# A bidirectional GLA and pooling block on one core: small vectors through ScalarE's queue, the first weights split before the features, output stores put off

## The chip, the core and the metric

The kernel runs on one core of a Trainium2 chip. Five engines work side by side, each through its own list of instructions in order: TensorE (PE; its weight loads are shown as PEld), VectorE (DVE), ScalarE (ACT), GpSimd (POOL) and SyncE (SP), which here only issues DMAs. An engine that meets an instruction whose semaphore has not been reached stands there, and everything behind it in its list stands too. The metric is the device time of one execution in microseconds (us). Lower is better.

## The reference

One layer on a sequence of 1024 tokens of 1024 features, in float32:

```python
h = rmsnorm(x, norm_mix[l])
proj = h @ w_in[l]
q, k, v, r, lr_f, lr_b, u, g_a, g_b = jnp.split(proj, split_points, axis=-1)
...
o = o_fwd + o_bwd                       # gated linear attention, 4 heads, both directions
o = o * lax.rsqrt(jnp.mean(o * o, axis=-1, keepdims=True) + EPS)
...
y_a = o @ w_branch_gla[l]
...
merged = jax.nn.sigmoid(g_a) * y_a + jax.nn.sigmoid(g_b) * y_b
x = x + merged @ w_out[l]
h2 = rmsnorm(x, norm_ffn[l])
gate, up = jnp.split(h2 @ w_ffn_in[l], 2, axis=-1)
x = x + (jax.nn.silu(gate) * up) @ w_ffn_out[l]
return rmsnorm(x, norm_final)
```

## The kernel before

All large products are made from a high and a low part of each operand: `split_to` casts a tile on ACT (line 196, outputs `wh`, `hh`, `oh`: high) and subtracts the cast from the source on DVE or POOL (line 197, outputs `wl`, `hl`, `ol`: low). Three matmuls (`products`, line 270) then stand for one. TensorE is busy nearly all the time, and the rest of the program is arranged beside it.

**Order of the work.** The program is written out by hand: each engine does its instructions in the order in which the Python code emits them. Work beside the products is emitted by `pump`, which is called after each group of three matmuls and counts their cost. `soon(delay, step)` puts a step into the list `put_off`; `pump` lowers all the delays, and emits steps from the front of the list only, so that a step whose delay has passed still waits for the one ahead of it. `Weights` puts the splits of a loaded weight block into the list `pending`.

**The start.** The sequence is normed tile by tile: `norm_x(t)` makes the mean square of 128 tokens on ACT (`norm_scale`, line 310), adds EPS on DVE (line 301), raises to the power -0.5 on POOL (line 302), scales on DVE (line 306, output `xn`), and loads tile t + 4 into the place of tile t. TensorE transposes `xn` (line 317, output `tr`), and `gain_and_split` makes the features of two tiles from it, four times, each on a pair of feature blocks: ACT writes the high part with the norm's gain (line 324, `hh`), DVE the low part (line 327, `hl`). The gains come from six small vectors that are loaded into the 40 rows of one tile `rows`, transposed at line 410 and copied to `cols`. The first product, `values(w, v, 0)`, needs the four parts of its weights (`raw`, loaded as four DMAs of 256 KB) split, and the features of tiles 0 and 1; the second, `values(w, v, 1)`, has the transposes of tiles 2 and 3 after its first three matmuls.

**DMA completion semaphores.** The framework has eight semaphores for the ends of DMAs, `DMAHW0` to `DMAHW7`. It hands them out in turn to the DMAs of the whole program, whichever queue issues them. A DMA that gets a semaphore for the second time first waits, in the queue that issues it, until the DMA that had it before has landed. The tables of order below show these waits in brackets.

**The end.** The last product, of the FFN's output, is made in seven steps p (`OUT_ORDER`), each over six pieces; a piece is loaded as `wor` and `gor` by SP (lines 1641, 1643 and 1644) and split as above. `collect` adds a finished sum to the residual (line 1753). After step p = 3 the tiles 0 to 3 are whole: `whole(m)` squares them, and `soon` emits the scale (2 units later), the final norm (`finish`, line 1724, 1.5 units later) and, within `finish`, the store of the tile (line 1727). Steps 7 and 4 follow and finish tiles 4 to 7 (lines 1742 to 1747).

Of the kernel before, what the change touches and what calls it, by code (L numbers as in the profile page):

```python
# [15 lines left out]
ALU = mybir.AluOpType  # L16

P = 128
# [16 lines left out]
EPS = 1e-6  # L35
# [16 lines left out]
def kernel(  # L52
# [20 lines left out]
    nc = tc.nc  # L73
    x, out = x[0], out[0]
# [16 lines left out]
    def name(s):  # L91
        count[0] += 1
        return f"{s}_{count[0]}"

    def slot(dtype=F32, shape=(2, HALF), s="slot"):
        return slots.tile([P, *shape], dtype, tag="slot", name=name(s))
# [7 lines left out]
    def vec(width, s="v"):  # L104
        return small.tile([P, width], F32, tag="vec", name=name(s), bufs=12)
# [4 lines left out]
    def as_f32(ap):  # L110
        return ap.bitcast(F32)
# [8 lines left out]
        out=keepf[:, :P], in_=keepf[:, :P], compare_op=ALU.is_ge, fill=0.0,  # L120
# [25 lines left out]
    pending, credit = [], [0.0]  # L146
# [4 lines left out]
    def soon(delay, *steps):  # L151
        put_off.extend([delay, step] for step in steps)
# [42 lines left out]
    def split_to(hi, lo, src, eng=nc.vector):  # L195
        nc.scalar.copy(hi, src)  # L196
        eng.tensor_tensor(lo, src, as_f32(hi), op=ALU.subtract)  # L197
# [13 lines left out]
    class Weights:  # L211
# [8 lines left out]
        def split(self, raw):  # L220
            hi = wts.tile(list(raw.shape), F32R, tag="wh", name=name("wh"))[:, :, :]
            lo = wts.tile(list(raw.shape), F32R, tag="wl", name=name("wl"))[:, :, :]
            split_to(hi, lo, raw[:, :, :], nc.gpsimd if hT.tiles else nc.vector)
            self.parts.append((hi, lo))

        def finish(self):
# [15 lines left out]
    def fetch():  # L242
        src = next(order, None)
        if src is not None:
            loaded.append(load(*src))

    def prepare():
        if not loaded:
            fetch()
        if loaded:  # L250
            ready.append(Weights(loaded.pop(0)))

            credit[0] = -2.0
# [44 lines left out]

    def rms_scale(ms, width, s):
        rs = vec(width, s)  # L300
        nc.vector.tensor_scalar(rs[:, :], ms, EPS, None, op0=ALU.add)
        nc.gpsimd.tensor_tensor(rs[:, :], rs[:, :], half_neg[:, :width], op=ALU.pow)
        return rs

# [3 lines left out]
    def norm_scale(xt, sq, s):  # L308
        ms = vec(1, s + "ms")
        nc.scalar.activation(sq[:, :], xt, AF.Square, scale=1.0 / 32.0, accum_out=ms[:, :])  # L310
        return rms_scale(ms[:, :], 1, s + "rs")

    def transpose_tile(ps, xt, i, kp):
        for kk in range(2):
            c = slice((2 * kk + i) * P, (2 * kk + i + 1) * P)
            k = 2 * kp + kk
            nc.tensor.transpose(ps[:, c], xt[:, k * P : (k + 1) * P], ident[:, :])  # L317

    def gain_and_split(ps, kp, t0, act, gain):
        c = slice((t0 % 4) * P, (t0 % 4 + 2) * P)  # L320
        both = range(2 * kp, 2 * kp + 2)
        srcs = [(ps[:, i * 2 * P : (i + 1) * 2 * P], gain[:, k : k + 1]) for i, k in enumerate(both)]
        for k, (src, g) in zip(both, srcs):
            nc.scalar.activation(act(k, t0 // 4)[0][:, c], src, AF.Copy, scale=g)
        for k, (src, g) in zip(both, srcs):
            hi, lo = act(k, t0 // 4)
            nc.vector.scalar_tensor_tensor(
                lo[:, c], src, g, as_f32(hi[:, c]), op0=ALU.mult, op1=ALU.subtract
            )
# [11 lines left out]
    xt = [slot(shape=(D,), s="x") for _ in range(4)]  # L341
    xn = [slot(shape=(D,), s="xn") for _ in range(4)]
    vec_rows = [(norm_mix, 8), (norm_ffn, 8), (gla_norm, 8), (pool_scale, 8), (b_decay_fwd, 4), (b_decay_bwd, 4)]
    n_rows = sum(n for _, n in vec_rows)
    rows = tmp.tile([n_rows, P], F32, tag="t2", name="rows")
    uraw = slot(F32, (HEADS, 2, DK), "uraw")
    lraw = slot(F32, (KT, 2 * RANK), "lraw")

    def load_x(t):
        nc.sync.dma_start(xt[t % 4][:, :], x[t * P : (t + 1) * P, :])  # L350

    def load_rows(at, v, n):
        nc.sync.dma_start(rows[at : at + n, :], v[0].rearrange("(j p) -> j p", p=P))

    def load_up(i, d, w):
        r = 2 * RANK * i + RANK * d
        nc.sync.dma_start(uraw[r : r + RANK, :, d, :], w[0].rearrange("r (h c) -> r h c", h=HEADS))

    load_x(0)
    load_rows(0, *vec_rows[0])  # L360
    load_x(1)
    for i in range(1, len(vec_rows)):
        load_rows(sum(n for _, n in vec_rows[:i]), *vec_rows[i])
    fetch()
    for t in (2, 3):
        load_x(t)
# [3 lines left out]
    hT = Activations("h")  # L370
# [32 lines left out]
    def value_slots():  # L403
        return [(slot(F32R, (4, DV), "vh"), slot(F32R, (4, DV), "vl")) for _ in range(2)]

    v = value_slots()
# [10 lines left out]
    for t in range(2):  # L417
        for kp, ps in enumerate(trs):
            transpose_tile(ps, xn[t], t, kp)
    prepare()  # L420
    for kp, ps in enumerate(trs):
        pending.pop(0)()
        gain_and_split(ps, kp, 0, hT, g_mix)
    w = take(ahead=False)
    norm_x(2)
# [203 lines left out]
    def attention(h, q, k):  # L629
# [153 lines left out]
        for n in range(NT):  # L783
# [24 lines left out]
            if n == 3:  # L808
                p = q_next
            yield 1.02  # L810
        rs = rms_scale(ms[:, :], NT, "ors")
        if h == HEADS - 1:
            o_heads[h] = o
# [20 lines left out]
    for h in range(HEADS):  # L834
# [4 lines left out]
        if h > 0:  # L839
            v = value_slots()  # L840
# [641 lines left out]
    def squares(t, ms, res, j):  # L1482
        nc.scalar.activation(
            res[:, COLS[j]], x2[t][:, COLS[j]], AF.Square, scale=1.0 / 32.0, accum_out=ms[:, j : j + 1]
        )

    def two_scale(ms):
        rs = vec(1, "n3rs")
        nc.vector.tensor_scalar(rs[:, :], ms[:, 0:1], ms[:, 1:2], EPS, op0=ALU.add, op1=ALU.add)
        nc.gpsimd.tensor_tensor(rs[:, :], rs[:, :], half_neg[:, :1], op=ALU.pow)  # L1490
        return rs
# [220 lines left out]
    def whole(t):  # L1712

        ms, res = vec(4, "n3ms"), slot(shape=(D,), s="res")
        for j in range(2):
            squares(t, ms, res, j)

        def scale():
            rs = two_scale(ms)
            soon(1.5, partial(finish, rs))  # L1720

        def finish(rs):
            for j in range(2):
                nc.vector.scalar_tensor_tensor(
                    res[:, COLS[j]], x2[t][:, COLS[j]], rs[:, :], gain_final[:, COLS[j]], op0=ALU.mult, op1=ALU.mult
                )
            nc.sync.dma_start(out[t * P : (t + 1) * P, :], res[:, :])

        soon(2, scale)

# [43 lines left out]
    for at, p in enumerate(OUT_ORDER):  # L1774
# [4 lines left out]
        for i in range(CLOSE if closing else n_of):  # L1779
            n = at * n_of + i  # L1780
# [50 lines left out]
```

## Time and profile before

| | |
|---|---|
| median of 3 runs | 1402.03 us (1400.65 to 1402.65) |
| the profiled execution | 1400.65 us, its span 1398.9 us |
| TensorE busy | 1368.4 us, 98% of the span |
| VectorE, ScalarE, GpSimd busy | 849.5, 625.6, 748.3 us |
| TensorE clock granted | 0.999 |
| DMA | 243.62 MB, mean 174 GB/s |

Times in the rows are us from the start of the span, durations of single instructions ns where it says so. A row of the timeline gives start, duration, engine, line, operation, output and inputs, and in brackets how long the engine had stood idle before it and what ended that. Rows of merged instructions carry their number as xN. Matmuls overlap each other, so that a merged row is shorter than their sum.

### The profile page before, as it was taken

Reading aid. Unit: us, or ns where it says so; the run is one execution under the profiler, and the core shown is the slowest. Engines: PE = TensorE matmul, PEld = TensorE weight load, DVE = VectorE, ACT = ScalarE, POOL = GpSimd, SP = SyncE. Lnnn points to the kernel's source line nnn. Section 1 sums busy time; section 2 is a strip of 40 time slices with the busy share of each in tenths; the row PEclk is TensorE's granted clock in tenths of the full one; section 3 lists DMA queues with packets and bytes.
Section 4 is the critical chain, followed back from the end, with each engine's and each line's share of the span. In section 5 each row is a group of like instructions: output and inputs, shape, how many; then the busy total and the mean of one; then the engine's idle time right before and its main releaser. Section 6 shows DMA issues by size and latency. Waiting matters only on the chain.

```text
span 1398.9 us, 18565 instructions
## 1 busy us (share of the span) xinstructions
PE 1368.4 (98%) x6677; PEld 1152.5 (82%) x6677; DVE 849.5 (61%) x1073; ACT 625.6 (45%) x1117; POOL 748.3 (53%) x558
## 2 busy tenths in 40 slices
PE   7999999999999999999999999999999999999997
PEld 6889898978888878788887788888888888888876
DVE  6256757567745975687875865556565556343363
ACT  6364655564233444455346633333333334453253
POOL 3242626031378456568665176666666667454354
PEclk9999999999999999999999999999999999999999
DMA  6212404341268667996515455554444447975461
GB/s 193 76 45 61 136 37 137 102 125 53 76 199 281 213 209 232 354 404 244 200 71 180 166 181 174 173 173 159 145 141 149 140 154 254 388 255 218 165 234 67
DMA packets 167612, 243.62 MB, mean 174 GB/s; under 512 B 10936, under 2 KB 98016, under 8 KB 167520
## 3 DMA queue, kind: packets, MB, share of 16 engines
q1 hardware_dynamic: 167520, 242.45, 51.3%
q8 instruction: 52, 0.85, 0.2%
q14 instruction: 40, 0.33, 0.1%
HBM read 164.55 MB, written 77.86 MB: 173 GB/s over the span
## 4 chain that ended last, share of the span: by engine, by line
PE 81%; DVE 7%; ACT 3%; issue 3%; POOL 3%; DMA 2%; SPq 0%; POOLq 0%; DVEq 0%; ACTq 0%
PE ps L270 74%; PE op L797 2%; POOL wl L197 1%; PE kv L270 1%; PE sc L733 1%; PE op L270 1%; PE tr L317 1%; DMA u_out<-uph 1%; DVE z L666 1%; PE ps L448 1%; DVE fs L866 0%; DMA gor<-g_out 0%; DMA wor<-t_out 0%; DVE so L725 0%; ACT wh L196 0%
## 5 line engine op out<-in xcount | busy, mean ns | idle before, releaser
L197 POOL TENSOR_TENSOR wl<-fs,wh 128x512 fp32r<-128x512 f32 x120 | 166.1, 1388 | 164.8 <-ACT wh L196 139.5
L270 PE MATMUL ps<-gl,wh 128*128 128x512 f32 x616 | 239.8, 389 | 0.9 <-DVE gl L1423 0.9
L270 PE MATMUL ps<-gh,wh 128*128 128x512 f32 x616 | 240.4, 390 | 0.0
L270 PE MATMUL ps<-gh,wl 128*128 128x512 f32 x616 | 239.7, 389 | 0.0
L197 POOL TENSOR_TENSOR wl<-fraw,wh 128x512 fp32r<-128x512 f32 x90 | 129.2, 1436 | 58.2 <-ACT wh L196 57.8
L197 POOL TENSOR_TENSOR ol<-gor,oh 128x1024 fp32r<-128x1024 f32 (+1 forms) x42 | 100.3, 2394 | 93.1 <-ACT oh L196 84.7
L270 PE MATMUL ps<-hh,wh 128*128 128x512 f32 x376 | 149.8, 398 | 0.0
L270 PE MATMUL ps<-hh,wl 128*128 128x512 f32 x376 | 146.7, 390 | 0.0
L270 PE MATMUL ps<-hl,wh 128*128 128x512 f32 x376 | 146.5, 390 | 0.0
L197 POOL TENSOR_TENSOR wl<-raw,wh 128x512 fp32r<-128x512 f32 x47 | 66.3, 1423 | 147.6 <-ACT wh L196 139.2
L270 PEld LDWEIGHTS ps<-gl,wh 128*128 128x128 f32 x616 | 115.7, 188 | 24.9 <-DVE gl L1423 1.3
L270 PEld LDWEIGHTS ps<-gh,wl 128*128 128x128 f32 x616 | 115.7, 188 | 24.2
L270 PEld LDWEIGHTS ps<-gh,wh 128*128 128x128 f32 x616 | 115.7, 188 | 23.6
L270 PE MATMUL ps<-oh,oh 128*128 128x512 f32 x308 | 119.9, 389 | 1.2 <-DVE x L1753 1.2
L270 PE MATMUL ps<-ol,oh 128*128 128x512 f32 x308 | 120.0, 389 | 0.2 <-DVE ol L197 0.2
L270 PE MATMUL ps<-oh,ol 128*128 128x512 f32 x308 | 119.8, 389 | 0.0
L197 POOL TENSOR_TENSOR wl<-wraw,wh 128x512 fp32r<-128x512 f32 x56 | 89.9, 1633 | 45.0 <-ACT wh L196 44.9
L197 DVE TENSOR_TENSOR ol<-wor,oh 128x1024 fp32r<-128x1024 f32 (+1 forms) x42 | 62.0, 1496 | 54.4 <-ACT oh L196 47.1
L196 ACT CAST wh<-fs 128x512 fp32r<-128x512 f32 x120 | 73.8, 615 | 28.8 <-DVE fs L866 28.7
L270 PEld LDWEIGHTS ps<-hh,wl 128*128 128x128 f32 x376 | 70.6, 188 | 15.0
L270 PEld LDWEIGHTS ps<-hl,wh 128*128 128x128 f32 x376 | 70.7, 188 | 13.4
L270 PEld LDWEIGHTS ps<-hh,wh 128*128 128x128 f32 x376 | 70.7, 188 | 13.3
(249 smaller groups left out, 3183.1 us busy)
## 6 DMA issues: line engine op xcount, KB each, us to landing
fraw<-in_w_ffn_in_dram SPq DMA_DIRECT2D x44, 512.0 KB, 5.8
gor<-g_out SPq DMA_DIRECT2D x35, 512.0 KB, 6.7
raw<-in_w_in_dram SPq DMA_DIRECT2D x48, 256.0 KB, 3.0
g_out<-s SPq DMA_DIRECT2D x44, 256.0 KB, 2.3
fraw<-in_w_in_dram SPq DMA_DIRECT2D x20, 512.0 KB, 6.7
wor<-t_out SPq DMA_DIRECT2D x20, 512.0 KB
g_out<-g SPq DMA_DIRECT2D x33, 256.0 KB, 2.6
x<-in_x_dram SPq DMA_DIRECT2D x16, 512.0 KB, 5.1
```

What stands on the lines that cost most here:

```text
L196: nc.scalar.copy(hi, src)
L197: eng.tensor_tensor(lo, src, as_f32(hi), op=ALU.subtract)
L270: nc.tensor.matmul(ps, a[i], b[j], start=first and n == 0, stop=last and n == 2, skip_group_check=onto)
L317: nc.tensor.transpose(ps[:, c], xt[:, k * P : (k + 1) * P], ident[:, :])
L448: nc.tensor.matmul(ps[:, :], lw[k // 4][:, k % 4, :, :].rearrange("p a r -> p (a r)"), hT(k, half)[i], start=k == 0 and i == 0, stop=k == ...
L666: nc.vector.tensor_tensor_scan(cs[:, :], cy, la[:, :], 0.0, op0=ALU.mult, op1=ALU.add)
L733: nc.tensor.matmul(sc[d][:, i * CH : (i + 1) * CH], chunk_of(ke, n, d), chunk_of(qe, n, d), start=True, stop=True,)
L797: nc.tensor.matmul(op[:, :DV], a, b, start=False, stop=j == len(terms) - 1)
```

## The change

It has four parts.

1. The six small vectors are loaded by DMAs that ACT's queue issues. SP's queue issues the tiles of x, the weights and everything else, without those six.
2. The four splits of the first weight block are emitted ahead of the four `gain_and_split`s and not one before each, and their low parts go to DVE, POOL, DVE, POOL in turn; before, the first went to DVE and three to POOL.
3. `rms_scale` adds EPS on POOL instead of DVE. It serves the eight tiles at the start (`n1rs`) and the end of each of the four heads (`ors`).
4. The stores of tiles 0 to 3 are put off by nine units of `pump` after the final norm.

```diff
         def split(self, raw):
             hi = wts.tile(list(raw.shape), F32R, tag="wh", name=name("wh"))[:, :, :]
             lo = wts.tile(list(raw.shape), F32R, tag="wl", name=name("wl"))[:, :, :]
-            split_to(hi, lo, raw[:, :, :], nc.gpsimd if hT.tiles else nc.vector)
+
+            split_to(hi, lo, raw[:, :, :], nc.vector if not hT.tiles and len(self.parts) % 2 == 0 else nc.gpsimd)
             self.parts.append((hi, lo))
...
         rs = vec(width, s)
-        nc.vector.tensor_scalar(rs[:, :], ms, EPS, None, op0=ALU.add)
+        nc.gpsimd.tensor_scalar(rs[:, :], ms, EPS, None, op0=ALU.add)
         nc.gpsimd.tensor_tensor(rs[:, :], rs[:, :], half_neg[:, :width], op=ALU.pow)
...
-    def load_x(t):
-        nc.sync.dma_start(xt[t % 4][:, :], x[t * P : (t + 1) * P, :])
+    def load_x(t, eng=nc.sync):
+        eng.dma_start(xt[t % 4][:, :], x[t * P : (t + 1) * P, :])
 
     def load_rows(at, v, n):
-        nc.sync.dma_start(rows[at : at + n, :], v[0].rearrange("(j p) -> j p", p=P))
+        nc.scalar.dma_start(rows[at : at + n, :], v[0].rearrange("(j p) -> j p", p=P))
...
     load_x(0)
-    load_rows(0, *vec_rows[0])
     load_x(1)
-    for i in range(1, len(vec_rows)):
+    for i in range(len(vec_rows)):
         load_rows(sum(n for _, n in vec_rows[:i]), *vec_rows[i])
     fetch()
...
     prepare()
+    while pending:
+        pending.pop(0)()
     for kp, ps in enumerate(trs):
-        pending.pop(0)()
         gain_and_split(ps, kp, 0, hT, g_mix)
...
-            nc.sync.dma_start(out[t * P : (t + 1) * P, :], res[:, :])
+            soon(9, partial(nc.sync.dma_start, out[t * P : (t + 1) * P, :], res[:, :]))
```

**ACT at the start of the program.** The rows are the first instructions of ACT's list, each with the semaphores that it waits for; `rows` are the small vectors, `x_126` and `x_127` the first two tiles, `tr` the transposes. Before:

```order
L310 ACT_TABLE_LOAD
L310 ACTIVATE xn_130,n1ms_164<-x_126 128x1024 [waits DMAHW0_49]
L310 ACTIVATE xn_131,n1ms_175<-x_127 128x1024 [waits DMAHW2_49]
L196 CAST wh_202<-raw_145 128x512 [waits DMAHW0_49]
L324 ACTIVATE hh_206<-tr_182,cols 128x256 [waits DVE_49,PE_49]
L324 ACTIVATE hh_206<-tr_182,cols 128x256
L196 CAST wh_212<-raw_147 128x512 [waits DMAHW1_49]
```

and now:

```order
L354 DMA rows<-in_norm_mix_dram 8x128
L354 DMA rows<-in_norm_ffn_dram 8x128 [waits DMAHW0_49]
L354 DMA rows<-in_gla_norm_dram 8x128 [waits DMAHW2_49]
L354 DMA rows<-in_pool_scale_dram 8x128 [waits DMAHW3_49]
L354 DMA rows<-in_b_decay_fwd_dram 4x128 [waits DMAHW4_49]
L354 DMA rows<-in_b_decay_bwd_dram 4x128 [waits DMAHW6_49]
L311 ACT_TABLE_LOAD
L311 ACTIVATE xn_130,n1ms_164<-x_126 128x1024
L311 ACTIVATE xn_131,n1ms_175<-x_127 128x1024 [waits DMAHW1_49]
L196 CAST wh_202<-raw_145 128x512
L196 CAST wh_206<-raw_147 128x512
```

Six DMAs stand ahead of the table load and the squares of the first tile, five of them with a wait, and the casts of the weights now follow each other.

**SP at the start.** These are the first DMAs of SP's list; `raw` are the four parts of the first weights, `x_128` and `x_129` tiles 2 and 3. Before:

```order
L350 DMA x_126<-in_x_dram 128x1024
L353 DMA rows<-in_norm_mix_dram 8x128
L350 DMA x_127<-in_x_dram 128x1024
...
L204 DMA raw_145<-in_w_in_dram 128x2x256 [waits DMAHW0_49]
L204 DMA raw_147<-in_w_in_dram 128x2x256 [waits DMAHW1_49]
L204 DMA raw_149<-in_w_in_dram 128x2x256 [waits DMAHW2_49]
L204 DMA raw_151<-in_w_in_dram 128x2x256 [waits DMAHW3_49]
L350 DMA x_128<-in_x_dram 128x1024 [waits DMAHW4_49]
L350 DMA x_129<-in_x_dram 128x1024 [waits DMAHW5_49]
```

and now:

```order
L351 DMA x_126<-in_x_dram 128x1024
L351 DMA x_127<-in_x_dram 128x1024
L204 DMA raw_145<-in_w_in_dram 128x2x256
L204 DMA raw_147<-in_w_in_dram 128x2x256
L204 DMA raw_149<-in_w_in_dram 128x2x256
L204 DMA raw_151<-in_w_in_dram 128x2x256
L351 DMA x_128<-in_x_dram 128x1024
L351 DMA x_129<-in_x_dram 128x1024 [waits DMAHW1_49]
L367 DMA lraw_136<-in_w_in_dram 128x8x32 [waits DMAHW5_49]
```

SP's first seven DMAs wait for nothing now. They hold the semaphores 0 to 6 in this order: x tile 0 has 0, tile 1 has 1, the four `raw` have 2 to 5, and tile 2 (`x_128`) has 6. The first of the six small vectors got 7, and the other five got 0, 2, 3, 4 and 6, each the second to have it.

**DVE near the end of the program.** The rows are the final norms of tiles 2 and 3 (`res_11921`, `res_11932`) and the low parts of two pieces (`ol`). Before:

```order
L1724 SCALAR_TENSOR_TENSOR res_11902<-x_2141_10890,n3rs_11927,gfin_10843 128x512 x2
L1489 TENSOR_SCALAR n3rs_11954<-n3ms_11931 128x1
L1724 SCALAR_TENSOR_TENSOR res_11921<-x_2148_10928,n3rs_11945,gfin_10843 128x512 x2
L1724 SCALAR_TENSOR_TENSOR res_11932<-x_2155_10966,n3rs_11954,gfin_10843 128x512 x2
L197 TENSOR_TENSOR ol_11970<-wor_11886,oh_11969 128x1024
L197 TENSOR_TENSOR ol_12006<-wor_11936,oh_12005 128x1024
```

and now:

```order
L1725 SCALAR_TENSOR_TENSOR res_11902<-x_2141_10890,n3rs_11927,gfin_10843 128x512 x2
L1490 TENSOR_SCALAR n3rs_11952<-n3ms_11931 128x1
L197 TENSOR_TENSOR ol_11962<-wor_11886,oh_11961 128x1024
L1725 SCALAR_TENSOR_TENSOR res_11921<-x_2148_10928,n3rs_11944,gfin_10843 128x512 x2
L1725 SCALAR_TENSOR_TENSOR res_11932<-x_2155_10966,n3rs_11952,gfin_10843 128x512 x2
L197 TENSOR_TENSOR ol_12004<-wor_11936,oh_12003 128x1024
```

One low part stands ahead of two final norms now, because the put-off stores of tiles 0 and 1 hold up the list of `put_off`. On SP the four stores stood together ahead of the loads of the last piece of step 7. Now that piece's two loads come first, then the stores of tiles 0 and 1, the two loads of the first piece of step 4, and the stores of tiles 2 and 3. TensorE's list is the same in both kernels.

## The prediction

> **What bounds the kernel now.** I read the share of busy time first, then the waits of TensorE one by one, then the chain of waits in the two places that the change touches. The busy shares and two stretches of the span:
>
> ```profile
> PE 1368.4 (98%) x6677; PEld 1152.5 (82%) x6677; DVE 849.5 (61%) x1073; ACT 625.6 (45%) x1117; POOL 748.3 (53%) x558
> ...
> 0.00:19.05 19.05, 8.94 (x50) 7.43 (x51) 10.61 (x25) 12.67 (x24) 9.43 (x45) 1.00 0.76 236
> 19.05:1330.00 1310.95, 1298.70 (x6365) 1095.82 (x6365) 804.08 (x1008) 583.11 (x1043) 702.37 (x492) 1.00 0.52 174
> ```
>
> TensorE is busy 98% of the span at full clock. Of its 30.5 us of idle time, 10.1 lie in the first 19.05 us. The change adds and removes nothing on TensorE, so it can move only idle time: a delay at the start shifts all that follows, since the 1311 us after it are 99% TensorE, and a gain is worth at most what TensorE waits there. The chain of waits through the start:
>
> ```profile
> 0.80 3.70 DMA x<-in_x_dram
> 4.53 1.16 ACT xn L310 x2
> 5.71 0.17 DVE n1rs L301
> ...
> 6.60 0.76 DVE xn L306
> 7.41 2.42 PE tr L317 x10
> 9.85 0.84 ACT hh L324 x2
> 10.69 0.51 ACT wh L196
> ...
> 13.69 0.74 ACT hh L324 x2
> 14.43 1.04 ACT xn L310 x2
> ...
> 17.21 0.56 POOL n1rs L302
> 17.80 0.38 DVE xn L306
> ```
>
> The first tile lands at 4.50, its square starts at 4.53, the first high part `hh` at 9.85. From there ACT is the chain: four pairs of `hh` with three weight casts of 0.51 between them, then the squares of tiles 2 and 3. TensorE's last wait of the start is for the norm of tile 3:
>
> ```profile
> 18.61 0.44 PE L317 MATMUL tr<-ident,xn 128*128 128x128 f32 x2 [1.04 <-DVE n1rs L301]
> ```
>
> So the time of this transpose, 18.61, is what the first three parts of the change move. Behind it TensorE is fed.
>
> **Part 1, the small vectors on ACT's queue.** SP loses six issues. The timeline of SP and of ACT:
>
> ```profile
> 0.80 0.39 SPq L350 DMA_DIRECT2D x<-in_x_dram  x1
> 1.25 0.36 SPq L353 DMA_DIRECT2D rows<-in_norm_mix_dram  x1
> 1.66 0.36 SPq L350 DMA_DIRECT2D x<-in_x_dram  x1
> ...
> 3.45 0.29 SPq L353 DMA_DIRECT2D rows<-in_b_decay_bwd_dram  x1
> 4.52 2.66 SPq L204 DMA_DIRECT2D raw<-in_w_in_dram  x4
> ...
> 0.80 1.28 ACT L310 ACT_TABLE_LOAD   x1 [0.80 <-PEq L1817]
> 4.53 1.06 ACT L310 ACTIVATE xn<-x 128x1024 f32<-128x1024 f32 x1 [2.45 <-DMA x<-in_x_dram]
> ...
> 14.28 1.10 ACT L310 ACTIVATE xn<-x 128x1024 f32<-128x1024 f32 x1
> ...
> 16.27 0.24 ACT L310 ACTIVATION_READ_ACCUMULATOR xn<-x 128x1 f32 x1
> ```
>
> The last small vector's issue ends at 3.74, but the first `raw` goes out at 4.52. It is the ninth DMA, gets the semaphore that tile 0 had, and tile 0 lands at 4.50: SP stood until then. The waits of SP's queue in the first 20 us name it:
>
> ```profile
> SPq L204 <- DMA x<-in_x_dram: 1.6, 2, 0.8
> ```
>
> The same rule now holds on ACT. By the order shown above, five of its six DMAs wait for semaphores, and these are held by SP's first DMAs: for tile 0, for three of the `raw`, and the last one, `b_decay_bwd`, for tile 2 (`x_128`, semaphore 6). ACT works in order, so its table load and the square of tile 0 stand behind the landing of tile 2, which nothing in the mathematics asks for.
>
> When does tile 2 land? SP issues it as its seventh DMA without a wait, at about 0.80 + 6 x 0.43 = 3.4, with the 0.43 from one issue to the next that SP's first three rows show. Its bytes stand behind tiles 0 and 1 (1049 KB) and the `raw` (1049 KB). What the DMA engines moved in the first 20 us, in slices of 0.5 us:
>
> ```profile
> GB/s 0 0 0 66 147 221 410 356 356 352 181 150 301 365 279 127 274 322 238 305 319 352 279 319 357 294 302 349 388 374 410 303 115 49 25 8 115 180 319 361
> ```
>
> The first eleven slices sum to 1044 KB, so tiles 0 and 1 are through at 5.5. With the queue full (10.0 to 15.5) the mean is 340 GB/s. I let the next 1573 KB, the `raw` and tile 2, start at 5.3 and move at 330: 4.8 us, to 10.1. A landing is told 0.6 us after the bytes (tile 0's 524 KB are through at 3.9, and it lands at 4.50). So tile 2 lands at 10.7. The early bound is the best slice, 410 GB/s from 5.5 on, with 0.5 us: 9.8. The late bound is the longest landing in this stretch, 8.0 us from issue, as the row below says for all eight tiles: 11.4. I keep 10.7, the estimate from the filled queue.
>
> ```profile
> DMA to landing us min/median/max: 3.7/5.1/8.0
> ```
>
> Then follow the last issue, 0.30 (as on SP), the table load, 1.28, and three hops of together 0.09: the square of tile 0 starts at 12.37 and not at 4.53, 7.84 later. The chain up to the first `hh` (2 squares beside it, transposes, hops) keeps its 5.32 us: `hh` at 17.69. The tile `rows` is complete at the latest 3.7 us after the last issue (what the first tile's 512 KB take), by 14.7, and the copy to `cols` stands behind `xn` on DVE, which ends near 15.2: hidden.
>
> **Part 2, the splits ahead.** The squares end at about 14.6, the four casts take 4 x 0.51, until 16.7: hidden under the transposes that `hh` waits for until 17.69. So the three casts between the pairs of `hh` leave the chain: -1.53. The low parts:
>
> ```profile
> L197 POOL TENSOR_TENSOR wl<-raw,wh 128x512 fp32r<-128x512 f32 x47 | 66.3, 1423 | 147.6 <-ACT wh L196 139.2
> ```
>
> POOL's two at 1.4 end by 19, while the fourth block's product, behind the fourth pair of `hh`, comes after 20; DVE's two end before the first pair of `hh` is there, near 18.5. Both are hidden.
>
> **Part 3, EPS on POOL.** DVE's 0.15 and the hop from DVE to POOL go, a POOL instruction of 128x1 comes. No row shows an add of this size on POOL. The nearest are
>
> ```profile
> L690 POOL TENSOR_TENSOR fac<-fac x16: 192/204/1139, 87.6 to 301.1; 128x4 f32<-128x4 f32 x16
> L302 POOL TENSOR_TENSOR n1rs<-n1rs,half_neg 128x1 f32<-128x1 f32 x8 | 4.4, 550 | 12.5 <-DVE n1rs L301 12.5
> ```
>
> a multiply of 128x4 at 0.20 and the power at 0.55. I take 0.2, the plainer operation; the ends are 0.1 and 0.55. For tile 0 that is even with before (0.91 from the square's end to `xn`). For tile 3 something goes: DVE's add stood behind the scaling of tile 2, so that `xn` of tile 3 started 17.80 - 16.51 = 1.29 after its square. Without DVE in between it is 0.2 + 0.56 and three hops of together 0.16, or 0.92: -0.37. At the ends of the heads the same 0.2 replaces 0.17, on no chain that TensorE waits for: 0, with 0.3 either way.
>
> Together: `hh` at 17.69, the squares of tiles 2 and 3 at 17.69 + 4.43 - 1.53 = 20.59, their end 2.23 later at 22.82, `xn` of tile 3 at 23.74, its transpose 0.81 later at 24.55. Against 18.61 this is **+5.9 us**. The later tiles do not catch up: tile 4's load waits for tile 0's scaling, but has from 15.3 to 22.8 to land, and the semaphores are as before from tile 4 on.
>
> **Part 4, the stores put off.** The timeline of SP and DVE, and TensorE's only two waits after 1330:
>
> ```profile
> 1337.40 8.83 SPq L1727 DMA_DIRECT2D out_dram<-res  x4
> 1346.32 0.38 SPq L1643 DMA_DIRECT2D wor<-t_out  x1
> ...
> 1338.86 7.01 DVE L1724 SCALAR_TENSOR_TENSOR res<-x,n3rs,gfin 128x512 f32<-128x512 f32 x4
> 1345.80 2.35 DVE L197 TENSOR_TENSOR ol<-wor,oh 128x1024 fp32r<-128x1024 f32 x2
> ...
> 1357.20 2.20 DVE L197 TENSOR_TENSOR ol<-wor,oh 128x1024 fp32r<-128x1024 f32 x1 [1.30 <-ACT oh L196]
> 1359.33 1.27 DVE L1753 TENSOR_TENSOR x<-ps,x 128x512 f32<-128x512 f32 x2
> ...
> 1347.06 0.50 PE L270 MATMUL ps<-ol,oh 128*128 128x512 f32 x1 [0.23 <-DVE ol L197]
> 1364.67 0.50 PE L270 MATMUL ps<-oh,oh 128*128 128x512 f32 x1 [1.20 <-DVE x L1753]
> ```
>
> One `ol` now stands ahead of the four slow norms (7.01 us for four), so the 0.23 goes. The next piece's loads no longer stand behind the stores, so the splits near 1357 come earlier and the sums at 1359.33 can start some 0.5 sooner, which takes about 0.5 off the 1.20. The rest stays: the third sum stands behind another `ol`. I take **-0.7**, with ends 0 (the later loads still set it) and -1.43 (both waits gone). The loads of step 4's second piece go out behind tile 3's store, as before, but with two pieces fewer between, so not later.
>
> **Sum.** +5.9 - 0.7 = +5.2 us. On the profiled execution's own 1400.65 that is 1405.9; it lies 1.38 under the median of the runs, so on the median it is 1402.03 + 5.2 = **1407.2 us**, +0.37%.
>
> A rule that could add to it: the Trainium skill (ScalarE: Activation LUTs, "What ACT_TABLE_LOAD costs") puts about 1.38 us of draining beside the 1.28 of the load. With it the sum would be 1408.6. The trace speaks against it: a load in the middle of the program has its first user right behind it,
>
> ```profile
> 270.96 1.28 ACT L654
> ...
> 272.25 2.05 ACT z L654 x4
> ```
>
> so the sum goes without.
>
> **The rivals.** (a) *ACT is not held.* The six issues would take 6 x 0.34 = 2.0 us on ACT, the table load would end at 4.2, before tile 0 lands, and SP would issue the weights 2.9 us sooner. Then parts 2 and 3 pay alone: -1.5 - 0.4 at the start, -0.7 at the end, 1399.4; with the whole of the end 1398.7. Only this gives a gain. The Trainium skill has its rule (DMA: Bandwidth & Descriptors, "Issuing engines are not separate DMA queues": issuing from several engines only saves a sequencer's time for the issue), and by it alone this is what one would expect. Against it speak SP's 0.8 us at 4.52 and the list of ACT. It decides by tile 2's landing L: the net is L - 5.5, so a gain would need L under 5.5, when only tiles 0 and 1 are through. (b) *Tile 2 lands late*, after 12, if the DMA engines run unevenly (the slices from 16 to 18 trail at 115 to 8 GB/s): each us is one more; at 13 it gives 1409.5. (c) *The start is hidden or made up*: some 3 us of the delay would have to be regained, so that the net is within 0.2% (2.8 us, which is what a measurement of this kernel can just tell from no change). The place would be tile 2's landing near 8.3; that needs 1573 KB at 520 GB/s, above every slice. Time about 1404.5.
>
> **How the numbers follow.** Forecast with L from 9.8 to 11.4: 0.80; (b) 0.10; (c) 0.06; (a) 0.04. The range: L's bounds give -0.9 and +0.7, the end's +0.7 and -0.7, POOL's add +0.35, the heads 0.3, and the three runs stand up to 1.4 under and 0.6 over their median. Taken together, with (b) partly in, 1404.2 to 1409.6. Faster by over 0.2%: 0.03. Within: 0.07. Slower: 0.90.
>
> **What would show it.** Right: ACT's first square near 12.4 with tile 2's landing or a small vector's DMA as what it waits for, and TensorE's first transpose near 15.3; the casts `wh` in one run of four; TensorE's wait at the second pair of tiles ending near 24.5; at the end no wait at the former 1347, and a shorter one at 1364. Wrong: a first square at 4.5, or tile 2 landing outside 9.8 to 11.4; or waits of TensorE between 25 and 1330 us that before did not have.

## The result and the profile after

| | before | after |
|---|---|---|
| median, six runs each | 1402.28 us (1400.65 to 1402.65) | 1407.17 us (1406.68 to 1407.69) |
| ratio of the times, 95% interval | | 1.0041 (1.0031 to 1.0051) |
| profiled execution, its span | 1400.65 us, 1398.9 us | 1407.68 us, 1406.0 us |
| TensorE busy | 1368.4 us | 1368.0 us |
| first square on ScalarE | 4.53 | 12.32 |
| first scaled features `hh` | 9.85 | 18.54 |
| tile 3's transposes on TensorE | 18.61 | 25.93 |
| a product's wait in the FFN, far behind the start | 779.38 | 787.02 |
| last wait of TensorE | 1364.67 | 1371.65 |

The kernel became slower by 4.9 us in the medians and by 7.03 us between the two profiled executions. The difference between these two numbers is taken up with **b_stores** below. TensorE does the same work in the same time; what grew is its idle time at the start. The timeline of ScalarE (ACT) in the first 24 us of after:

```profile
0.80 0.58 ACTq L354 DMA_DIRECT2D rows<-in_norm_mix_dram  x1
4.65 0.28 ACTq L354 DMA_DIRECT2D rows<-in_norm_ffn_dram  x1
...
10.74 0.25 ACTq L354 DMA_DIRECT2D rows<-in_b_decay_bwd_dram  x1
11.03 1.28 ACT L311 ACT_TABLE_LOAD   x1 [11.03 <-DMA rows<-in_gla_norm_dram]
12.32 1.06 ACT L311 ACTIVATE xn<-x 128x1024 f32<-128x1024 f32 x1
...
14.42 2.16 ACT L196 CAST wh<-raw 128x512 fp32r<-128x512 f32 x4
18.54 3.02 ACT L325 ACTIVATE hh<-tr,cols 128x256 fp32r<-128x256 f32 x8 [1.97 <-PE tr L318]
21.41 1.11 ACT L311 ACTIVATE xn<-x 128x1024 f32<-128x1024 f32 x1
...
23.40 0.24 ACT L311 ACTIVATION_READ_ACCUMULATOR xn<-x 128x1 f32 x1
```

The six loads are strung out from 0.80 to 10.74, and the table load and the first square stand behind the last of them. What each load waited for can be read from the trace's record of the DMA semaphores. Tile 0 was complete on its semaphore at 4.63, three of the `raw` at 6.60, 7.92 and 8.65, and tile 2 at 10.72; ScalarE's five waiting loads went out at 4.65, 6.62, 7.94, 8.67 and 10.74, each 0.02 after the landing of the DMA that had its semaphore before. The four casts now follow each other in 2.16. The timeline of TensorE, only the rows before which it waited (the wait and what ended it in brackets):

```profile
15.28 1.97 PE L318 MATMUL tr<-ident,xn 128*128 128x128 f32 x8 [2.10 <-DVE xn L307]
17.82 1.56 PE L318 MATMUL tr<-ident,xn 128*128 128x128 f32 x8 [0.56 <-DVE xn L307]
...
25.93 0.44 PE L318 MATMUL tr<-ident,xn 128*128 128x128 f32 x2 [1.08 <-DVE xn L307]
...
787.02 0.50 PE L271 MATMUL ps<-gl,wh 128*128 128x512 f32 x1 [0.87 <-DVE gl L1424]
...
1371.65 0.50 PE L271 MATMUL ps<-oh,oh 128*128 128x512 f32 x1 [1.09 <-DVE x L1754]
```

The first transposes start at 15.28 instead of 7.41. The wait at 787.02 is this one of before,

```profile
779.38 0.50 PE L270 MATMUL ps<-gl,wh 128*128 128x512 f32 x1 [0.87 <-DVE gl L1423]
```

7.64 later and of the same length: nothing was made up on the way. The shift is 7.32 at tile 3 and even grows near 568, where after waits twice for loads of `p_out` (0.70 and 0.66) and before once (0.95). At the end the wait at 1347 is gone, and the last one shrank from 1.20 to 1.09, and the shift falls from 7.64 to 6.98. The wait at 1347 had cost more than its row says: the matmuls there started 0.62 and 0.34 apart where their neighbours are 0.23 apart, which is 0.50 in all. VectorE and GpSimd at the start of after, from their timelines:

```profile
14.47 0.75 DVE L307 TENSOR_SCALAR xn<-x,n1rs 128x1024 f32<-128x1024 f32 x1 [9.61 <-POOL n1rs L303]
16.00 1.76 DVE L307 TENSOR_SCALAR xn<-x,n1rs 128x1024 f32<-128x1024 f32 x1 [0.67 <-POOL n1rs L303]
...
25.12 0.75 DVE L307 TENSOR_SCALAR xn<-x,n1rs 128x1024 f32<-128x1024 f32 x1 [0.77 <-POOL n1rs L303]
...
15.93 2.96 POOL L197 TENSOR_TENSOR wl<-raw,wh 128x512 fp32r<-128x512 f32 x2
22.69 0.22 POOL L302 TENSOR_SCALAR n1rs<-n1ms 128x1 f32<-128x1 f32 x1 [3.80 <-ACT xn L311]
23.73 0.70 POOL L302 TENSOR_SCALAR n1rs<-n1ms 128x1 f32<-128x1 f32 x1 [0.17 <-ACT xn L311]
```

The scaling of tile 1 takes 1.76 where that of tile 0 takes 0.75; GpSimd subtracts low parts at the same time. GpSimd's addition of EPS takes 0.22 alone and 0.70 while VectorE scales a tile. Neither shape is slow in the start of before, but the same thing can be seen near its end, on VectorE and GpSimd:

```profile
1337.41 1.41 DVE L1724 SCALAR_TENSOR_TENSOR res<-x,n3rs,gfin 128x512 f32<-128x512 f32 x2
...
1339.98 5.34 POOL L197 TENSOR_TENSOR ol<-gor,oh 128x1024 fp32r<-128x1024 f32 x2
```

Two final norms take 1.41 there, and the four that follow from 1338.86 take 7.01, 1.75 each, while GpSimd subtracts until 1345.32.

### The profile page after: what moved, and what is told of

It is laid out like the page before. It is cut to its first block, busy times and chain, and to the rows that moved or that the text cites. A ratio compares the mean times of both kernels' runs of the same rounds, so it can differ in the third digit from the quotient of the medians.

```text
span 1406.0 us, 18562 instructions
## 1 busy us (share of the span) xinstructions
PE 1368.0 (97%) x6677; PEld 1152.3 (82%) x6677; DVE 852.1 (61%) x1062; ACT 625.8 (45%) x1117; POOL 753.0 (54%) x569
```

## The experiments

Two theories stood against each other. The theory of the prediction: ScalarE is held by its last small load, which waits for a semaphore that a tile of the features still has. The rival: the cost lies in parts 2 and 3, in the casts put ahead and in GpSimd working beside VectorE. A second profile of the kernel before goes with the first four as a control.

**before_again**: no edit.

> The kernel before, a second time, for what two profiles of one kernel differ by. Every theory: 1402.3 us; the first square on ScalarE at about 4.5, tile 3's transposes at about 18.6, the end at 1398.9 to 1401 of the span.

Measured: 1402.57 us, ratio 1.0004 (0.9995 to 1.0013). Up to 513 us its rows agree with those of the first profile within 0.1 us, tile 3's transposes to the hundredth, 18.61. From there it falls back: 0.37 at a wait for a load of `p_out` near 568, and 0.46 in the last 585 us, where the wait at 1347 is 0.77 and not 0.23. So two profiles of one kernel can differ by 0.83 us in these two places. The first profile of before is the lowest of the runs shown with it, but at the end it was not lucky: its 585.29 from 779.38 on is the mean of the kernels without part 4 (585.25, under b_stores).

**a_rows_sp**: after without part 1.

```diff
-        nc.scalar.dma_start(rows[at : at + n, :], v[0].rearrange("(j p) -> j p", p=P))
+        nc.sync.dma_start(rows[at : at + n, :], v[0].rearrange("(j p) -> j p", p=P))
...
     load_x(0)
+    load_rows(0, *vec_rows[0])
     load_x(1)
-    for i in range(len(vec_rows)):
+    for i in range(1, len(vec_rows)):
```

> After, with the six vectors back on SyncE's queue in the old order; the weights' splits, EPS and the stores stay as in after. Theory (ScalarE is held by its sixth vector load, which waits for a completion semaphore that a tile of the features still has): first square back at 4.5, the first scaled features hh at about 10.6, tile 3's transposes at about 18.1, 1401.5 us, faster than before by a little. Rival (the cost lies in the casts put ahead and in what now runs on GpSimd beside VectorE): about 1407.

**b_rows_act**: the inverse edit, part 1 alone, on before.

> Before, with the six vectors on ScalarE's queue and nothing else. Theory: first square at about 12.3, hh at about 17.6, tile 3's transposes at about 26.4, so +7.8 us: 1410.1. Rival (casts and GpSimd): 1402.3, as before.

Measured: a_rows_sp 1400.40 us, 0.9986 (0.9978 to 0.9995); b_rows_act 1408.86 us, 1.0047 (1.0033 to 1.0061); before beside them had 1402.29. They came out 1.1 and 1.2 us under their expectations. Part 1 carries the loss, whichever kernel it is put into or taken from, and the rest of the change by itself is a small gain. From b_rows_act, the timelines of ScalarE and of TensorE's waits:

```profile
10.69 0.25 ACTq L353 DMA_DIRECT2D rows<-in_b_decay_bwd_dram  x1
10.97 1.28 ACT L310 ACT_TABLE_LOAD   x1 [10.97 <-DMA x<-in_x_dram]
12.27 1.06 ACT L310 ACTIVATE xn<-x 128x1024 f32<-128x1024 f32 x1
...
26.35 0.44 PE L317 MATMUL tr<-ident,xn 128*128 128x128 f32 x2 [1.04 <-DVE n1rs L301]
```

Tile 3's transposes are 7.74 later than in before, and the trace names a load of `x` as what ScalarE waited for. The same two views of a_rows_sp:

```profile
4.76 1.06 ACT L311 ACTIVATE xn<-x 128x1024 f32<-128x1024 f32 x1 [2.68 <-DMA x<-in_x_dram]
...
11.86 0.62 ACT L196 CAST wh<-raw 128x512 fp32r<-128x512 f32 x1 [1.33 <-DMA raw<-in_w_in_dram]
12.38 3.03 ACT L325 ACTIVATE hh<-tr,cols 128x256 fp32r<-128x256 f32 x8
...
19.78 0.44 PE L318 MATMUL tr<-ident,xn 128*128 128x128 f32 x2 [0.98 <-DVE xn L307]
```

The first square is back, but my expectation for the transposes, 18.1, missed: with ScalarE free, the casts ahead wait for the fourth raw weight, and `hh` comes at 12.38 instead of 9.85. That is 2.53 later, of which the casts now out of the way give back 1.53, and EPS on GpSimd costs 0.19; the sum, 1.19, is what the row shows (19.78 - 18.61 = 1.17). By 300 us most of this delay is gone from the trace, since a wait of 0.83 at 230 has vanished. VectorE shows why, in before and then in a_rows_sp:

```profile
225.18 1.48 DVE L725 TENSOR_SCALAR so<-st,fac 128x256 f32<-128x256 f32 x1
...
226.41 0.36 DVE L727 TENSOR_SCALAR so<-st,fac 128x256 f32<-128x256 f32 x1
```

In before this instruction starts in the middle of two subtractions on GpSimd (223.96 to 226.51) and ends just behind them, at 226.66; here it starts 0.19 before their end (226.60), and the 1.12 that it saves make up for the late start. That GpSimd is what slowed it is read from these rows, and no run tests it at this place. Of the other profiles only that of c_warm, below, has this gain.

**a_act3** and **a_act1**: a dose. In after, only the first three vectors, or only the first one, go through ScalarE; the others go out on SyncE's queue behind the raw weights.

```diff
-    def load_rows(at, v, n):
-        nc.scalar.dma_start(rows[at : at + n, :], v[0].rearrange("(j p) -> j p", p=P))
+    def load_rows(at, v, n, eng=nc.scalar):
+        eng.dma_start(rows[at : at + n, :], v[0].rearrange("(j p) -> j p", p=P))
...
-    for i in range(len(vec_rows)):
+    for i in range(3):                     # a_act1: range(1)
         load_rows(sum(n for _, n in vec_rows[:i]), *vec_rows[i])
     fetch()
+    for i in range(3, len(vec_rows)):      # a_act1: range(1, ...)
+        load_rows(sum(n for _, n in vec_rows[:i]), *vec_rows[i], eng=nc.sync)
```

> After, with the first three vectors on ScalarE's queue and the last three on SyncE's, behind the four raw weights. Theory (it is the sixth that waits for a feature tile): ScalarE's last load is issued at about 6.6, the first square starts at about 8.2 instead of 12.3, tile 3's transposes at about 21.8 instead of 25.9, about 1403.1 us. Rival (casts and GpSimd): about 1407.

> After, with one vector on ScalarE's queue and the other five on SyncE's, behind the four raw weights. By the assignment of the eight completion semaphores ScalarE's one load has a fresh one. Theory (only the waits on reused semaphores cost): table load at about 1.4, first square at 4.5 to 4.8, about 1400.5 us, as with all six on SyncE. Rival (a load issued by ScalarE costs in itself): first square later than 5.5 and 1401.5 us or more.

Measured: a_act3 1403.95 us, 1.0014 (1.0005 to 1.0023), 0.8 over its forecast; a_act1 1401.91 us, 1.0007 (0.9997 to 1.0016). The rows of a_act3 (its last load on ScalarE, the table load, the first square, tile 3's transposes):

```profile
6.87 0.28 ACTq L354 DMA_DIRECT2D rows<-in_gla_norm_dram  x1
7.18 1.28 ACT L311 ACT_TABLE_LOAD   x1 [7.18 <-DMA raw<-in_w_in_dram]
8.47 1.06 ACT L311 ACTIVATE xn<-x 128x1024 f32<-128x1024 f32 x1
...
22.07 0.44 PE L318 MATMUL tr<-ident,xn 128*128 128x128 f32 x2 [0.39 <-DVE xn L307]
```

and of a_act1 (the table load, the first square, the transpose of the vectors):

```profile
1.41 1.28 ACT L311 ACT_TABLE_LOAD   x1 [1.41 <-PEq L1820]
4.52 1.06 ACT L311 ACTIVATE xn<-x 128x1024 f32<-128x1024 f32 x1 [1.82 <-DMA x<-in_x_dram]
...
10.08 0.30 PE L412 MATMUL vps<-ident,rows 40*128 40x40 f32 x1 [10.08 <-DMA rows<-in_b_decay_bwd_dram]
```

The square follows the last load on ScalarE by 1.6 us: 6.87 and 8.47, in after 10.74 and 12.32. What the last load waited for changed with its semaphore: here the first of the `raw`, complete at 6.85, in after tile 2. A load that has a fresh semaphore costs the square nothing (4.52), so it is the waiting and not the issuing. a_act1 is 1.4 us over its forecast, which was made after a_rows_sp. The five vectors now stand behind the raw weights and a semaphore each on SyncE, land at 10.08 instead of 7.2, and TensorE's transposes stand behind theirs; but this makes tile 3's transposes only 0.35 later than in a_rows_sp (20.13 for 19.78). Of the 1.1 between the spans of the two profiles (1400.0 and 1398.9), most of the rest is the wait near 230, which a_act1 has (0.82).

**a_no_eps**: after without part 3 (EPS back on VectorE). **a_lows_dve**: after with all four first low parts on VectorE.

```diff
# a_no_eps
-        nc.gpsimd.tensor_scalar(rs[:, :], ms, EPS, None, op0=ALU.add)
+        nc.vector.tensor_scalar(rs[:, :], ms, EPS, None, op0=ALU.add)
# a_lows_dve
-            split_to(hi, lo, raw[:, :, :], nc.vector if not hT.tiles and len(self.parts) % 2 == 0 else nc.gpsimd)
+            split_to(hi, lo, raw[:, :, :], nc.vector if not hT.tiles else nc.gpsimd)
```

> After, with the addition of EPS back on VectorE (part 3 undone). The prediction's step (0.37 gained on the way to tile 3's transposes): these at 26.3, 1407.5 us. Rival (GpSimd's addition takes 0.70 to 0.78 instead of 0.2 beside VectorE's scaling, so part 3 lost 0.2): transposes at 25.7, 1407.0 us.

> After, with all four first low parts on VectorE, so that GpSimd subtracts nothing while VectorE scales the second tile. Theory (the scaling took 1.76 instead of 0.75 because GpSimd works beside it): the second tile's xn takes 0.75 again, its transposes start at 17.0 instead of 17.8, hh at 17.7 instead of 18.5; the low halves hl then wait for four subtractions on VectorE, which gives back about as much: 1406.5 to 1407.7 us. Rival (the 1.76 has another cause): xn still takes 1.7 and hh starts at 18.5.

Measured: a_no_eps 1407.34 us, 1.0043 (1.0029 to 1.0057); the times don't tell it from after. Its rows of ScalarE, VectorE and TensorE:

```profile
12.14 1.06 ACT L311 ACTIVATE xn<-x 128x1024 f32<-128x1024 f32 x1
...
23.20 0.24 ACT L311 ACTIVATION_READ_ACCUMULATOR xn<-x 128x1 f32 x1
...
22.89 0.14 DVE L302 TENSOR_SCALAR n1rs<-n1ms 128x1 f32<-128x1 f32 x1
...
25.18 0.75 DVE L307 TENSOR_SCALAR xn<-x,n1rs 128x1024 f32<-128x1024 f32 x1 [0.67 <-POOL n1rs L303]
...
25.99 0.44 PE L318 MATMUL tr<-ident,xn 128*128 128x128 f32 x2 [1.04 <-DVE n1rs L302]
```

The transposes are 0.06 later than in after, where 0.37 later was expected by the prediction's step and 0.2 earlier by the rival, though the landing that frees ScalarE came 0.18 earlier (first square 12.14 for 12.32). From the first square on, part 3 gains 0.24 here: tile 3's scaling starts 25.18 - 23.44 = 1.74 behind its square, in after 25.12 - 23.64 = 1.48, since VectorE's addition stands behind the low halves `hl`, which end only at 22.9. Where VectorE is free the same part costs: 1.49 in a_rows_sp against 1.29 in before. So neither expectation had it right: the sign of part 3 depends on what VectorE has in hand.

a_lows_dve: 1407.64 us, 1.0045 (1.0031 to 1.0058). Here too the time says nothing; the rows (VectorE, ScalarE, TensorE, and a view of TensorE's busy time, instructions, granted clock, DMA share and GB/s by stretch) say two things:

```profile
15.73 0.76 DVE L307 TENSOR_SCALAR xn<-x,n1rs 128x1024 f32<-128x1024 f32 x1 [0.67 <-POOL n1rs L303]
...
17.44 3.03 ACT L325 ACTIVATE hh<-tr,cols 128x256 fp32r<-128x256 f32 x8 [1.13 <-PE tr L318]
...
24.83 0.44 PE L318 MATMUL tr<-ident,xn 128*128 128x128 f32 x2 [1.07 <-DVE xn L307]
...
24.00:29.50 5.50, 4.67 (x27) 0.69 0.72 214
```

With GpSimd not subtracting, tile 1's scaling is back at 0.76. Its first square was at 12.04, `hh` follows 5.40 later (6.22 in after), and the transposes 12.79 later (13.61 in after): 0.82 gained. So the 1.76 was GpSimd working beside VectorE. But this gain does not arrive: from 24 to 29.5 TensorE's granted clock is 0.69, and at the next common wait, near 107, this kernel is 0.44 behind after.

**b_stores**: before with part 4 alone.

```diff
-            nc.sync.dma_start(out[t * P : (t + 1) * P, :], res[:, :])
+            soon(9, partial(nc.sync.dma_start, out[t * P : (t + 1) * P, :], res[:, :]))
```

> Before, with the stores of the normed tiles put off (part 4) and nothing else. Theory (part 4 is worth what the profiles show between 779 us and the end, 0.65 to 1.1): the stall of TensorE at 1347 is gone, the end of the span comes 0.7 to 1.1 earlier, 1401.2 to 1401.6 us. Rival (what the kernel with the vectors back on SyncE gained over before comes from the casts and EPS, the stores give nothing): 1402.3. Third possibility (the whole gain is the stores'): 1400.4.

Measured: 1400.95 us, 0.9995 (0.9986 to 1.0004), by the time not told from no change (before beside it: 1401.92). The wait at 1347 is gone. The profiles are sharper than the times. From the FFN's wait (779.38 in before) to TensorE's last wait (1364.67), the nine profiles of kernels with part 4, here and below, have 584.59 to 584.67 us, the five without it (before, before_again, b_rows_act, b_splits, b_warm) 584.78 to 585.75, mean 585.25. Part 4 gives 0.6 us, and takes away a scatter of 1 us. The span of b_stores came out at 1399.6, longer than before's 1398.9, because of a stretch right behind the start (the view by stretches again):

```profile
18.00:20.00 2.00, 1.63 (x12) 0.84 0.69 244
20.00:22.00 2.00, 2.00 (x11) 0.50 0.87 267
22.00:24.00 2.00, 2.00 (x16) 0.81 0.38 104
```

The clock is halved for 2 x (0.16 + 0.50 + 0.19) / 0.5 = 3.4 us, which costs 1.7 us of matmul time. I call this a spell. From tile 3's transposes to the wait near 100 us the profiles of all kernels fall into two groups: 80.73 to 80.81 (before, before_again, after and eight more) and 82.29 to 82.33 (b_stores, a_lows_dve, c_two_ahead). Such a spell there costs 1.5 us. a_rows_sp and b_splits have one too, earlier, from 14 to 18; TensorE still waited 0.98 and 0.71 for tile 3 behind it, and they are in the first group.

This is a candidate for most of the 2.1 us by which the profiled difference exceeds that of the medians: before's profiled execution lies 1.63 under its median, after's 0.51 over its own. The mean granted clock of each execution of before in these experiments speaks for it: 34 at 0.999 have a median of 1400.85 us, 49 at 0.998 one of 1402.24 us. But 0.998 alone doesn't prove a spell. The clock is at half as well for the last 2.6 us of before's span and the last 4.8 us of after's, behind TensorE's last matmul, and the profiled execution of after is at 0.998 without a spell. At 0.999 there is no room for one: 3.4 us of spell and the shortest such end of these profiles, 2.1, take 2.75 us from 1400 and leave 0.998. Of after's six executions five were at 0.999, and the sixth is the profiled one, so none had a spell like these.

**b_warm**: before, with TensorE kept busy in the two waits (0.80 and 1.04) ahead of the spell, by seven transposes whose results are overwritten.

```diff
             for i in range(2):
+                for _ in range(3 + i if (kp, t0, act) == (0, 2, hT) else 0):
+                    nc.tensor.transpose(ps[:, i * P : (i + 1) * P], ident[:, :], ident[:, :])
                 transpose_tile(ps, xn[i], i, kp)
```

**b_splits**: before with part 2 alone. **c_two_ahead**: before with part 4 and two of the four casts ahead. **c_warm**: c_two_ahead with the edit of b_warm.

```diff
# c_two_ahead and c_warm
+    for _ in range(2):
+        pending.pop(0)()
     for kp, ps in enumerate(trs):
-        pending.pop(0)()
+        if pending:
+            pending.pop(0)()
         gain_and_split(ps, kp, 0, hT, g_mix)
```

> Before, with seven throwaway transposes of the identity put on TensorE where it waits for tiles 2 and 3 of the features (three in the wait of 0.80, four in that of 1.04); they write where the real ones write right after. Theory C (most executions of before have a spell of some 3.4 us at half the granted clock, after a stretch in which TensorE waited for much of 3.4 us; the profiled one had none, which is why it lies 1.5 under the median): with the waits filled the spells become rarer, the median falls to 1400.7 to 1401.2 and the scatter shrinks. Rival (the scatter comes from the stores and other transfers): 1402.2 and as wide as before, or a little more for the transposes.

> Before, with part 2 alone (all four casts ahead, low parts on two engines). The prediction had 1.53 for it where the raw weights have landed; here the fourth raw weight lands at about 9.5 to 12, so the first hh waits for its cast: hh at about 12.4 instead of 9.8, the stalls for low parts gone (1.0): tile 3's transposes at 19 to 20, 1402.0 to 1403.5 us. Rival (part 2 gains its 1.53 here too): 1400.8.

> Before, with part 4 and two of the first four casts ahead of the features' scaling, the other two between as before; vectors on SyncE, EPS on VectorE. From the profile of before: TensorE's waits for low parts at 12.6, 13.9 and 15.1 (0.46, 0.27, 0.27) go, the stores give 0.7: 1400.6 us by the median of before, less if the clock stays up. Rival (the casts ahead delay hh, as with all four ahead): first hh later than 10.2, 1401.0 or more.

> The kernel of c_two_ahead (before, with part 4 and two of the first four casts ahead) with the seven throwaway transposes of b_warm, to see whether the gains add up. Theory: its spell-free executions (1398.8 to 1399.6) become the usual ones, 1399.0 to 1400.2 us, some 2 under before on the same chip. Rival (the gains don't add, since transfers take back what the head gains): 1400.9, as c_two_ahead.

| | median us | ratio to before, 95% interval | executions at clock 0.999 |
|---|---|---|---|
| b_warm | 1400.49 | 0.9994 (0.9985 to 1.0003) | 10 of 11 (before beside it: 13 of 27) |
| b_splits | 1401.15 | 0.9999 (0.9990 to 1.0008) | 4 of 10 |
| c_two_ahead | 1400.90 | 0.9997 (0.9988 to 1.0006) | 3 of 11 |
| c_warm | 1399.57 | 0.9986 (0.9977 to 0.9995) | 10 of 11 (before beside it: 6 of 15) |

The filled waits raise the clock: 10 of 11 executions at 0.999, in both kernels. The same stretch in c_warm, and two of TensorE's waits:

```profile
18.00:20.00 2.00, 1.98 (x17) 1.00 0.90 268
20.00:22.00 2.00, 2.00 (x20) 1.00 0.83 256
...
18.02 0.44 PE L317 MATMUL tr<-ident,xn 128*128 128x128 f32 x2 [0.61 <-DVE n1rs L301]
...
1362.42 0.50 PE L270 MATMUL ps<-oh,oh 128*128 128x512 f32 x1 [1.10 <-DVE x L1758]
```

b_warm's median fell by 0.8, a change that its interval doesn't separate from none, and its runs scatter as widely as those of before, so the spells are one cause of the scatter and not the only one. c_two_ahead has `hh` at 10.02 and tile 3's transposes at 17.73, 0.88 sooner than before, so its rival is out; but a spell begins at 17.7 in its profile, and its median is not told from before's. c_warm puts the parts together and is faster than before beside it (1401.53) by 2.0 us. Its profiled execution (1398.39) is not the typical one, as it has the gain of 1.1 near 230 that a_rows_sp has; without a profile of the others it can't be said how much of the 2.0 is this. b_splits has `hh` at 12.12 and the transposes at 19.32, as expected, but its 1401.15 lies under the 1402.0 to 1403.5 that it was given, and is no change that can be measured against before beside it (1401.31). The rival's 1400.8 is not excluded by the time, but its gain of 1.53 is by the rows.

## Why the prediction was right, and what in it was not

The forecast was 1407.2 with a range of 1404.2 to 1409.6; 1407.17 was measured. The mechanism is the predicted one. That the number agrees to 0.1 us is in part luck, as the steps show:

- **ScalarE held until tile 2 lands: right, to a tenth.** Predicted: last issue at 10.7, first square at 12.37, first transposes near 15.3, `rows` complete by 14.7. Measured: 10.74, 12.32, 15.28, and 12.89 for the transpose of the vectors. Part 1 alone costs 7.74 at tile 3 (b_rows_act), against the 7.84 of the sum. That the hold is the wait on semaphores is shown by the dose, and that tile 2's landing ends it by its semaphore, complete at 10.72 in after and at 10.66 in b_rows_act, where the last loads went out at 10.74 and 10.69.
- **The table load's drain: the trace was the better guide.** The load starts at 11.03, and the square follows 1.29 later; the 1.38 us more that the Trainium skill (ScalarE: Activation LUTs, "What ACT_TABLE_LOAD costs") would add are not there.
- **The casts ahead, -1.53: right for the held start alone.** The squares of tile 2 follow `hh` by 2.87 (21.41 - 18.54), predicted 2.90. In a start that isn't held, part 2 delays tile 3 by 0.71 instead (b_splits), as the casts then wait for their weights.
- **"Both are hidden", for the low parts: this step failed.** They were weighed for when they would be needed, and not for what they do to the engine beside them. GpSimd's two run while VectorE scales tile 1, which takes 1.0 longer and brings `hh` 0.85 late (18.54 for 17.69). a_lows_dve shows it. A price for it stood in the prediction's own lines: the "four slow norms" of 7.01 us run beside a subtraction on GpSimd, as the row above shows.
- **EPS on GpSimd, -0.37 with 0.2 for the addition: mis-sized.** Alone the addition takes 0.22 to 0.23, as taken, but for tile 3 it stands beside VectorE's scaling of tile 2 and takes 0.70. From the square's end to tile 3's scaling it is 1.48, neither the 0.92 of the sum nor the 1.29 of before: +0.19. Undone, it would be 1.74 here (a_no_eps), which the sum had not seen either, as it let the low halves end in time.
- **The sum at the start, +5.9: too small by 1.4.** 7.74 - 1.53 + 0.85 + 0.19 is 7.25; the rows have 7.32.
- **The stores, -0.7: right as a sum, by two errors.** It is 0.66 between the two profiles and 0.6 over all. But the wait at 1347, put at 0.23, gave 0.50, and the last wait, which was to give 0.5, gave 0.11.
- **The base.** The sum was put on the median of before, in part of whose executions, as far as the clock tells, there is a spell that the profiled one lacked. The executions of after had none. So most of the 1.4 us that the start costs more than predicted does not show in the medians, which are 4.9 apart where 5.2 was forecast; the agreement comes from these two cancelling, and nothing in the prediction foresaw it. At a clock of 0.999 the medians are 1400.85 and 1407.00, 6.15 apart, and after's profiled execution, at 1407.68, lies 0.7 over its own; this makes the 7.03 of the profiles, but for 0.2. Where in the unprofiled executions the clock was low, no trace shows.
- **The rivals.** (a), ScalarE not held, is excluded by the first square at 12.32. The nearest kernel in which it isn't held, a_rows_sp (its weights are issued no sooner, as the rival had it), came to 1400.40, where the rival had 1399.4; parts 2 and 3 delay tile 3 there by 1.17 and don't bring it forward by 1.9. Its profile ends 0.9 sooner than that of before_again: the 1.17 are regained at 230, and the rest is gained at the end, which is part 4's. Its median lies 1.9 under that of before beside it, and 8 of its 11 executions were at a clock of 0.999 against 7 of 27 of before; that spells are the other 1 us is likely and was not tested. (b) and (c) are excluded by the landing at 10.72 and by the shift of 7.64 that is still whole at 787 us. One sign that the prediction named as being wrong did show: a wait between 25 and 1330 that before did not have, the second one for `p_out`. before_again has it too, so it is not of the change.

## What to carry to other kernels

Before a DMA is moved to the queue of an engine that computes, look up which completion semaphore it will get and whose landing frees it: the whole engine waits for that landing, and a queue that only issues DMAs can bear it where a busy one can't. Work moved to an engine that has time is not free for its neighbour: price it by a row in which both run. And before a sum is put on a median, look whether the profiled execution is a typical one: a second profile of the same kernel and the granted clock by stretch help to tell.

## What was not expected of the hardware

- VectorE's scaling of 128x1024 float32 takes 0.75 us alone and 1.76 us beside GpSimd's subtraction of 128x512; GpSimd's addition on 128x1 takes 0.22 alone and 0.70 to 0.78 beside that scaling. Final norms of 128x512 take 0.71 each without a subtraction beside them and 1.75 each with one. The Trainium skill (SBUF — State Buffer, "Who interferes with whom") has a port pair that these two engines share and lock; the traces agree in kind, in both directions.
- TensorE's clock was granted at half for spells of 3.4 us in the start (and in every profile behind the last matmul, where nothing needs it): in b_stores from 19.4 on, behind 3.4 us in which TensorE had waited for 0.80 and 1.04, and not in every execution with the same waits (before). The Trainium skill (TensorE: Matmul & The Clock Gate, "What's actually happening") has a halved clock after an idle window of about 3.4 us, which runs freely; the length and the half agree, while TensorE here had worked for nearly half of the time. A spell cost 1.5 us where TensorE was the bound, and nothing that shows where it waited behind it. With seven throwaway transposes 10 of 11 executions were at 0.999, where 13 of 27 and 6 of 15 of before were.
- The first DMA that ScalarE issued took it 0.58 us, the later ones 0.25 to 0.28.
